# Eight k tiles of a feed-forward output projection as 2x2x2 block products with seven multiplications

## Chip, cores and metric

The kernel runs on one core of a Trainium2 chip. The metric is the device time of one execution in microseconds (us). All matrix products work in float32 accuracy: each operand is split into a high part, rounded for TensorE, and a low part, the remainder, and a product is made of three matmuls (high by high, high by low, low by high).

## What is computed

One layer of a decoder: a mixer sublayer (stick-breaking attention and a gated convolution), a cross-attention into 256 memory tokens, and a feed-forward sublayer (SwiGLU), each with a residual add, then a last RMSNorm. 512 tokens, 1024 channels, a hidden width of 2816. The change lies in the last product of the feed-forward sublayer:

```python
hf = rms_norm(x, norm_ffn[l])
gate, up = jnp.split(hf @ w_ffn_in[l], 2, axis=-1)
x = x + (jax.nn.silu(gate) * up) @ w_ffn_out[l]
...
return rms_norm(x, norm_final)
```

## The kernel before

Activations lie transposed: channels on the 128 partitions, 512 tokens along the free axis. A "tile" of channels is 128 of them: there are 8 tiles of model channels (`KD`) and 22 of the hidden width (`NF`).

**The tools of the kernel.** `load_w` brings a weight tile of 128x1024 by a DMA on SyncE's queue into a buffer `wr`, rounds it on ScalarE into `wh` (line 150) and takes the remainder on VectorE into `wl` (line 151). There are four buffers of each. `mm3` issues the three matmuls of a product (lines 155 to 157). `split` and `act_parts` make the high and low parts of activations, the cast on ScalarE, the remainder on VectorE. The buffers named `u` (50 of them, 128x512) hold activations and their forms.

**The input stage of the feed-forward sublayer** (up to about 729 us of the profile) already works with 2x2x2 blocks and seven products. A block is a pair of channel tiles by the two halves of the tokens (`HS` = 256) on one side and a pair of channel tiles by gate and up columns on the other. `forms_of` makes from two activation tiles the seven operands (sums and differences of quarters, VectorE, then split); `ffn_load` brings the weights of a block with three DMAs on SyncE's queue and one on GpSimd's that accumulates, so that two sums of weights are made by the DMA; `ffn_raw` makes two further sums on VectorE; `ffn_form` splits one operand into the buffers of `wh` and `wl` (which it shares with `load_w`): products 0 and 1 share a pair of buffers, the others take one buffer each, in turn from `wh` and from `wl`. `product` issues the twelve matmuls of 256 columns of one product (four k, three terms; line 803). Products 0, 3, 4 and 5 add up in one PSUM bank `z`; product 1 has a bank `v`; products 2 and 6 share a bank `y`. In between the values of `z` are copied out, since the outputs need partial sums of it.

The list `uses` gives the order over blocks m and products i: products of two neighbouring blocks alternate, so that between two products into the same `z` there is another one. The loop over it is hand-ordered on TensorE, ScalarE and VectorE (`manual_schedule`): these instructions keep their order among themselves, while instructions from outside the block may be put between them. At place n of the list the form of the product six places later is made (`AHEAD`) and the sum of the one eight places later (`SUM_AHEAD`).

**The output projection** (about 727 to 850 us) takes all eight PSUM banks as sums `acc[m]`, one for each tile of model channels: two from the pool of `v`, four from that of `z`, two from that of `y`; in the order m = 0 to 7 they are v, v, z, z, y, y, z, z. For each k tile, `out_step` issues for each m the three matmuls of 512 columns. That goes over the first 18 k tiles. The last four (`HOLD`) are held in all four weight buffers and worked half of the tokens by half (256 columns), in a hand-ordered block with the last norm and the output; its first nine products are the first three held tiles for m = 0 to 2. The residual `x2T[m]` (scaled beforehand, as the last norm is applied behind) is added there, when the sum of a half of one m is whole (line 983).

Of the kernel before, what the change touches and what calls it, by code (L numbers as in the profile page):

```python
# [11 lines left out]
ALU = mybir.AluOpType  # L12
# [14 lines left out]
HS = S // 2  # L27
EPS = 1e-6
HOLD = 4
MEM_AT = (5, 7, 9, 11)  # L30
MEAN_AT = 14
EARLY = 2
# [6 lines left out]

@with_exitstack  # L40
def hybrid_layer(ctx: ExitStack, tc: tile.TileContext, xT_d, memT_d, cols_d, wv_d, win_d,
                 wbr_d, wmix_d, wmq_d, wmk_d, wmv_d, wmo_d, wfi_d, wfo_d, out):
    nc = tc.nc

    cpool = ctx.enter_context(tc.tile_pool(name="cpool", bufs=1))
# [26 lines left out]
    def mmtile(s, pool=None, tag="mm"):  # L72
        return (pool or pmm).tile([P, 512], F32, tag=tag, name=nm(s))

    def ztile(s):
        return mmtile(s, pz, "z")
# [671 lines left out]

    def ffn_load(m):

        a = wfi_d[m].rearrange("p (i c) -> p i c", i=4)
        s13, wg = ((fpool, "wg") if (m % 3, t) in ((1, "ws"), (2, "wg")) else (wpool, "wr")
                   for t in ("ws", "wg"))
        s13 = s13[0].tile([P, 2, 512], F32, tag=s13[1], name=nm("ws"))
        nc.sync.dma_start(s13, a[:, 2:3, :].broadcast_to([P, 2, 512]))
        wg = wg[0].tile([P, 2, 512], F32, tag=wg[1], name=nm("wg"))
        nc.sync.dma_start(wg, a[:, 0:2, :])
        a22 = fpool.tile([P, 512], F32, tag="w2", name=nm("a22"), bufs=4)
        nc.sync.dma_start(a22, a[:, 3, :])
        nc.gpsimd.dma_start(s13, a[:, 0:4:3, :], accum_op=ALU.add)  # L760
        pairs[m] = wg
        raws[m] = [wg[:, 0, :], wg[:, 1, :], s13[:, 1, :], None, s13[:, 0, :], a22, None]
# [33 lines left out]
    def product(ps, m, i, ks=range(KP)):  # L796

        w = wforms[m, i]
        for k in ks:
            hi, lo = (w[j][:, k * P:(k + 1) * P] for j in range(2))  # L800
            xh, xl = x2f[k][i]
            for j, (a, b) in enumerate(((hi, xh), (hi, xl), (lo, xh))):
                nc.tensor.matmul(ps[:, :HS], a, b, start=i < 3 and k == 0 and j == 0,  # L803
                                 stop=k == KP - 1 and j == 2, skip_group_check=True)
# [43 lines left out]
                                                           in1=g[:, sl], op0=ALU.mult,  # L848
                                                           op1=ALU.mult))

    uses = [(0, 0), (0, 1), (0, 2)]
    for m in range(NF):
        if m < NF - 2:
            uses += [(m, 3), (m + 1, 0), (m, 4), (m + 1, 1), (m, 5), (m + 1, 2), (m, 6)]
        elif m == NF - 2:
            uses += [(m, 3), (m + 1, 0), (m, 4), (m + 1, 1), (m + 1, 2), (m + 1, 3), (m, 5),
                     (m + 1, 4), (m, 6), (m + 1, 5), (m + 1, 6)]
    actp = {}
    r2b = [None]

# [66 lines left out]
        evict(NF - 1, 2)  # L927


    acc = [mmtile("f") for _ in range(2)] + [ztile("f") for _ in range(4)]  # L930
    acc[4:4] = [otile("f") for _ in range(2)]

    def out_step(m, k, w, sl):
        fs = slice(m * P, (m + 1) * P)
        mm3(acc[m][:, sl], (w[0][:, 0, fs], w[1][:, 0, fs]), (actp[k][0][:, sl], actp[k][1][:, sl]),
            k == 0, k == NF - 1, skip_group_check=True)

    for k in range(NF - HOLD):
        w = load_w(wfo_d[k], D)
        if k + SCALED < NF:  # L940
            act_parts(k + SCALED, lows[-1:] + stts[-1:])
        for m in range(KD):
            out_step(m, k, w, slice(0, S))
    for k in range(NF - HOLD + SCALED, NF):
        act_parts(k, lows[-1:])
    held = [load_w(wfo_d[k], D) for k in range(NF - HOLD, NF)]
    tables = log_exp_tables(casts[-1])
    hs = HS
    halves = [slice(i * hs, (i + 1) * hs) for i in range(2)]
# [21 lines left out]
    with tc.manual_schedule(engines={mybir.EngineType.PE, mybir.EngineType.Activation,  # L971
                                     mybir.EngineType.DVE}):

        for m in range(3):
            for i in range(HOLD - 1):
                out_step(m, NF - HOLD + i, held[i], halves[0])
        for n in range(2 * KD):
            half, m = divmod(n, KD)
            sl = halves[half]
            for i in range(HOLD - 1 if n < 3 else 0, HOLD):  # L980
                out_step(m, NF - HOLD + i, held[i], sl)
            y = x2T[m][:, sl]
            nc.vector.tensor_tensor(out=y, in0=acc[m][:, sl], in1=y, op=ALU.add)
            if n > 0:
                add_square(*divmod(n - 1, KD))
            if n == 0:
                nc.vector.tensor_copy(v0, eps_sq[:, sl])
            elif n == KD:
                nc.vector.memset(v1, 0.0)
                parts = split(sq[0, 0], "sq", cols=hs)  # L990
            elif n == KD + 1:

                nc.vector.scalar_tensor_tensor(out=sq[1, 0], in0=eps_sq[:, sl], scalar=D / P,
                                               in1=sq[1, 0], op0=ALU.mult, op1=ALU.add)
            elif n == KD + 2:
                for i, part in enumerate(parts):
                    nc.tensor.matmul(v0, mean_r, part, start=False, stop=i == 1,
                                     skip_group_check=True)
            elif n == KD + 3:
                rf0 = rstd_of(v0, hs, "rf", tables, eps=False)  # L1000

            sq[half, m] = (acc[m][:, halves[0]] if half and 0 < m < KD - 2 else tmp("sq", hs))
            nc.scalar.activation(sq[half, m], y, AF.Square)
            if m % 2 == 0:
                yg[half, m // 2] = f(unit("yg")).rearrange("p (j t) -> p j t", j=2)
            nc.scalar.activation(yg[half, m // 2][:, m % 2, :], y, AF.Copy,
                                 scale=g_fin[:, m:m + 1])
        mean_of(0)
        mean_of(KD - 2)
        for m in range(2):  # L1010
            turn(m)
        mean_of(KD - 1)
        for m in range(2, KD):
            turn(m)
        r1 = rstd_of(v1.rearrange("p (c two) -> p c two", two=2)[:, :, 0], 2, "rt", tables,
                     eps=False)
        for j in range(2):
            for c in range(2):
                o, ps = f(unit("out")), acc[2 * j + c]
                if c == 0:  # L1020
                    nc.scalar.activation(o, ps, AF.Copy, scale=r1[:, 0:1])
                else:
                    nc.vector.tensor_scalar(out=o, in0=ps, scalar1=r1[:, 1:2], scalar2=None,
                                            op0=ALU.mult)
                q = nc.scalar if (j, c) == (1, 0) else nc.sync
                q.dma_start(out[1].rearrange("(c p d) -> c p d", c=2, d=D)[
                    c, :, j * 512:(j + 1) * 512], o)
# [12 lines left out]
def _layout(x, mem, norm_mix, w_in, conv_w, w_branch_a, w_branch_b, w_mix_out, norm_mem_q,  # L1040
            norm_mem_kv, w_mem_q, w_mem_kv, w_mem_o, norm_ffn, w_ffn_in, w_ffn_out, norm_final):
    import numpy as np

    def by_column(w, cols=P, k=KD):

        n = w.shape[1] // cols
        return w.reshape(k, P, n, cols).transpose(2, 1, 0, 3).reshape(n, P, k * cols)

    def by_row(w):

        return w.reshape(4, 2, P, 512).transpose(0, 2, 1, 3).reshape(4, P, 1024)

    def by_pair(w):


        return w.reshape(KD // 2, 2, P, 2, NF, P).transpose(4, 2, 3, 1, 0, 5).reshape(NF, P, 2048)

    gains = np.stack([norm_mix[0], norm_mem_q[0], norm_mem_kv[0], norm_ffn[0], norm_final])
    columns = np.concatenate([gains.reshape(5 * KD, P), conv_w[0].reshape(3 * TT, P)])
    arrays = {  # L1060
        "xT": x[0].T,
        "memT": mem[0].T,
        "columns": columns.T,
        "w_value": by_row(w_in[0][:, O_V:O_V + SBW]),
        "w_in": by_column(w_in[0]),
        "w_branch": np.concatenate([by_column(w_branch_a[0], k=4), by_column(w_branch_b[0], k=4)],
                                   axis=2),
        "w_mix_out": by_column(w_mix_out[0]),
        "w_mem_q": by_column(w_mem_q[0]),
        "w_mem_k": by_column(w_mem_kv[0][:, :D]),  # L1070
        "w_mem_v": np.stack([by_row(w_mem_kv[0][:, D + 512 * n:D + 512 * (n + 1)])
                             for n in range(2)]),
        "w_mem_o": by_column(w_mem_o[0]),
        "w_ffn_in": by_pair(w_ffn_in[0]),
        "w_ffn_out": w_ffn_out[0].reshape(NF, P, D),
    }
    return {f"in_{n}_dram": np.ascontiguousarray(a) for n, a in arrays.items()}

# [17 lines left out]
```

## Time and profile before

| | us |
|---|---|
| median of 3 runs | 859.74 (859.27 to 860.23) |
| the profiled execution, its own time | 859.25 |
| its span, first to last instruction | 857.5 |
| TensorE busy | 850.1 |
| VectorE busy | 585.9 |
| ScalarE busy | 430.7 |

The profile is one execution. PE is TensorE's matmuls, PEld its weight loads (beside the matmuls), DVE is VectorE, ACT ScalarE, POOL GpSimd, SP SyncE. "L803" is line 803 of the kernel. A group of instructions reads: line, engine, operation, output<-input tile, shapes, count | busy us in all, mean ns of one | idle time of the engine just before them and what ended it. In the timeline the first two numbers are start and length in us; neighbouring instructions of one engine overlap by a little, so the distance of two starts is what an instruction costs in a row, and the length is somewhat more.

### The profile page before, as it was taken

How to read it: one execution, taken by the hardware profiler on the slowest of the kernel's cores; microseconds unless marked ns; L12 is line 12 of the kernel's file. 1: busy time of each engine (PE TensorE's matmuls, PEld its weight loads, DVE VectorE, ACT ScalarE, POOL GpSimd, SP SyncE). 2: the span in 40 equal slices, each digit the busy share in tenths (PEclk: the TensorE clock that was granted, in tenths of full speed). 3: DMA queues.
4: the chain of work that ended last, by engine and by line, in shares of the span. 5: the costliest groups of instructions: out<-in, count | busy, mean ns of one | idle time of the engine just before them, and what ended most of it. 6: DMA issues, size and time to landing. Idle time of an engine off the chain costs nothing.

```text
span 857.5 us, 12690 instructions
## 1 busy us (share of the span) xinstructions
PE 850.1 (99%) x4912; PEld 748.4 (87%) x4912; DVE 585.9 (68%) x963; ACT 430.7 (50%) x750; POOL 64.5 (8%) x92
## 2 busy tenths in 40 slices
PE   9999999999999999999999999999999999999997
PEld 7878787888888898888888889999999999888897
DVE  9769889986454475555555789888877778533334
ACT  7465767664233344433434666554455556422335
POOL 1011112210000000000000101111111100000002
PEclk9999999999999999999999999999999999999999
DMA  8332232219333255333120527777777764332202
GB/s 296 134 112 87 87 111 87 74 59 296 112 105 112 91 172 191 128 98 99 50 74 25 142 56 196 192 176 176 189 185 195 181 147 135 111 99 99 73 1 99
DMA packets 42859, 108.34 MB, mean 126 GB/s; under 512 B 4656, under 2 KB 8752, under 8 KB 42800
## 3 DMA queue, kind: packets, MB, share of 16 engines
q1 hardware_dynamic: 36528, 95.72, 34.1%
q0 software_dynamic: 5984, 11.54, 8.3%
q8 instruction: 38, 0.62, 0.3%
q10 hardware_dynamic: 288, 0.29, 0.1%
q14 instruction: 21, 0.17, 0.1%
HBM read 104.36 MB, written 2.10 MB: 124 GB/s over the span
## 4 chain that ended last, share of the span: by engine, by line
PE 99%; DVE 0%; POOL 0%; issue 0%; DVEq 0%; ACT 0%; POOLq 0%
PE z L803 15%; PE pr L155 8%; PE pr L156 8%; PE pr L157 8%; PE y L803 7%; PE f L156 5%; PE f L155 5%; PE f L157 5%; PE v L803 4%; PE r L157 3%; PE r L156 3%; PE r L155 3%; PE v L261 3%; PE mq L157 2%; PE mq L155 2%; PE mq L156 2%
## 5 line engine op out<-in xcount | busy, mean ns | idle before, releaser
L150 ACT CAST wh<-wr 128x1024 fp32r<-128x1024 f32 x106 | 111.2, 1052 | 218.4 <-issue 98.6
L151 DVE TENSOR_TENSOR wl<-wr,wh 128x1024 fp32r<-128x1024 f32 x106 | 129.2, 1221 | 99.5 <-ACT wh L150 99.2
L155 PE MATMUL pr<-xgh,wh 128*128 128x512 f32 x288 | 112.6, 391 | 0.0
L156 PE MATMUL pr<-xgl,wh 128*128 128x512 f32 x288 | 112.3, 390 | 0.0
L157 PE MATMUL pr<-xgh,wl 128*128 128x512 f32 x288 | 112.3, 390 | 0.0
L156 PE MATMUL f<-actl,wh 128*128 128x512 f32 (+1 forms) x208 | 74.2, 357 | 0.0
L155 PE MATMUL f<-acth,wh 128*128 128x512 f32 (+1 forms) x208 | 74.2, 357 | 0.0
L157 PE MATMUL f<-acth,wl 128*128 128x512 f32 (+1 forms) x208 | 74.0, 357 | 0.0
L803 PE MATMUL z<-xdh,wf 128*128 128x256 f32 x352 | 70.3, 283 | 0.0
L157 PEld LDWEIGHTS pr<-xgh,wl 128*128 128x128 f32 x288 | 54.1, 188 | 11.4
L155 PEld LDWEIGHTS pr<-xgh,wh 128*128 128x128 f32 x288 | 54.1, 188 | 11.2 <-DVE rv L124 0.3
L156 PEld LDWEIGHTS pr<-xgl,wh 128*128 128x128 f32 x288 | 54.1, 188 | 10.8
L760 POOL DMA_DIRECT2D ws<-in_w_ffn_in_dram x22 | 26.6, 1208 | 468.0 <-DVE c L618 266.3
L803 PEld LDWEIGHTS z<-xdh,wf 128*128 128x128 f32 x352 | 58.0, 192 | 0.0
L823 ACT COPY sa<-z 128x256 f32<-128x256 f32 x44 | 16.4, 373 | 78.2 <-PE z L803 78.2
L803 PE MATMUL z<-xdl,wf 128*128 128x256 f32 x176 | 49.8, 283 | 0.0
L794 DVE TENSOR_TENSOR wf<-s,wf 128x512 fp32r<-128x512 f32 x44 | 30.3, 690 | 21.1 <-ACT wf L793 20.0
L155 PEld LDWEIGHTS f<-acth,wh 128*128 128x128 f32 x208 | 39.3, 189 | 5.8
L157 PEld LDWEIGHTS f<-acth,wl 128*128 128x128 f32 x208 | 39.3, 189 | 5.6
L156 PEld LDWEIGHTS f<-actl,wh 128*128 128x128 f32 x208 | 39.3, 189 | 5.5
L803 PE MATMUL y<-xch,wf 128*128 128x256 f32 x176 | 35.5, 283 | 0.0
L803 PE MATMUL v<-xoh,wf 128*128 128x256 f32 x176 | 35.5, 283 | 0.0
(281 smaller groups left out, 2135.5 us busy)
## 6 DMA issues: line engine op xcount, KB each, us to landing
wr<-in_w_in_dram SPq DMA_DIRECT2D x36, 512.0 KB, 3.4
ws<-in_w_ffn_in_dram SPq DMA_DIRECT2D x22, 512.0 KB, 3.8
wg<-in_w_ffn_in_dram SPq DMA_DIRECT2D x22, 512.0 KB, 4.3
ws<-in_w_ffn_in_dram POOLq DMA_DIRECT2D x22, 512.0 KB, 5.8
wr<-in_w_ffn_out_dram SPq DMA_DIRECT2D x22, 512.0 KB, 3.3
a<-in_w_ffn_in_dram SPq DMA_DIRECT2D x22, 256.0 KB, 4.5
wr<-in_w_branch_dram SPq DMA_DIRECT2D x8, 512.0 KB, 3.3
wr<-in_w_mem_k_dram SPq DMA_DIRECT2D x8, 512.0 KB, 3.3
```

The lines of the kernel that those rows point to most:

```text
L150: after(nc.scalar.copy(h2, raw), lead[-1:])
L151: lows.append(nc.vector.tensor_tensor(out=l2, in0=raw, in1=f(h2), op=ALU.subtract))
L155: nc.tensor.matmul(ps, a[0], b[0], start=start, stop=False, **kw)
L156: nc.tensor.matmul(ps, a[0], b[1], start=False, stop=False, **kw)
L157: nc.tensor.matmul(ps, a[1], b[0], start=False, stop=stop, **kw)
L261: nc.tensor.matmul(vps[t], xg[k][a][:, sl], wv[k][b], start=k == 0 and (a, b) == (0, 0), stop=k == KD - 1 and a == 1)
L760: nc.gpsimd.dma_start(s13, a[:, 0:4:3, :], accum_op=ALU.add)
L794: nc.vector.tensor_tensor(out=lo, in0=raw, in1=f(hi), op=ALU.subtract)
L803: nc.tensor.matmul(ps[:, :HS], a, b, start=i < 3 and k == 0 and j == 0, stop=k == KP - 1 and j == 2, skip_group_check=True)
L823: nc.scalar.copy((s[:, :HS], None, None, s[:, HS:], t[:, :HS])[i], z)
```

## The change

K tiles 10 to 17 of the output projection leave the plain loop, which now runs over the first ten (`TURN`). They become four pairs (`NT`) of k tiles; the eight output tiles become four pairs (`NB`); the tokens two halves. Each block, numbered 22 to 25 as a continuation of the blocks of the input stage, is one pair of output tiles over all four k pairs, in seven products with the same `product`, `ffn_form`, `ffn_raw` and `ffn_load`; the weights come from a new array laid out by blocks. The operands of the activations, `af`, are made by `forms_of` at k = 2, 4, 6 and 8 of the plain loop.

Behind the plain loop come the parts of the four held activation tiles and the first six places of the new order. Then, hand-ordered: eight adds move the sums of ten k tiles out of the banks into `x2T`; 28 products follow, each with a `part_of`, which adds its bank (or subtracts it) to one quarter of the block in `x2T`. Afterwards the eight banks are taken anew, the four held weight tiles are loaded, and the tail runs as before over the held tiles, now beginning new sums.

```diff
+TURN = 10
+NT = (NF - HOLD - TURN) // 2
+NB = D // (2 * P)
...
-        a = wfi_d[m].rearrange("p (i c) -> p i c", i=4)
+        a = (wfi_d[m] if m < NF else wfp_d[m - NF]).rearrange("p (i c) -> p i c", i=4)
...
-            xh, xl = x2f[k][i]
+            xh, xl = (x2f if m < NF else af)[k][i]
...
+    def order(m0, n):
+        u = [(m0, 0), (m0, 1), (m0, 2)]
+        for m in range(m0, m0 + n - 2):
+            u += [(m, 3), (m + 1, 0), (m, 4), (m + 1, 1), (m, 5), (m + 1, 2), (m, 6)]
+        m = m0 + n - 2
+        return u + [(m, 3), (m + 1, 0), (m, 4), (m + 1, 1), (m + 1, 2), (m + 1, 3), (m, 5),
+                    (m + 1, 4), (m, 6), (m + 1, 5), (m + 1, 6)]
+
+    uses = order(0, NF)
+    af = []
...
-    for k in range(NF - HOLD):
+    for k in range(TURN):
         w = load_w(wfo_d[k], D)
-        if k + SCALED < NF:
+        if k + SCALED < TURN:
             act_parts(k + SCALED, lows[-1:] + stts[-1:])
+        if k > 1 and k % 2 == 0 and len(af) < NT:
+            j = TURN + 2 * len(af)
+            af.append(forms_of(act[j], act[j + 1]))
         for m in range(KD):
-            out_step(m, k, w, slice(0, S))
-    for k in range(NF - HOLD + SCALED, NF):
+            out_step(m, k, w, slice(0, S), 0, TURN - 1)
+    for k in range(NF - HOLD, NF):
         act_parts(k, lows[-1:])
-    held = [load_w(wfo_d[k], D) for k in range(NF - HOLD, NF)]
+
+    def part_of(m, i):
+
+        z, v, y = (banks[m][t][:, :HS] if t in banks[m] else None for t in "zvy")
+        xa, xb = x2T[2 * (m - NF)], x2T[2 * (m - NF) + 1]
+        x, ps, sign = {0: (xa[:, :HS], z, 1), 1: (xa[:, :HS], v, 1), 2: (xb[:, HS:], y, -1),
+                       3: (xa[:, HS:], z, 1), 4: (xb[:, HS:], z, -1), 5: (xb[:, :HS], z, -1),
+                       6: (xa[:, HS:], y, 1)}[i]
+        if sign > 0:
+            nc.vector.tensor_tensor(out=x, in0=ps, in1=x, op=ALU.add)
+        else:
+            nc.vector.scalar_tensor_tensor(out=x, in0=ps, scalar=-1.0, in1=x, op0=ALU.mult,
+                                           op1=ALU.add)
+
+    turns = order(NF, NB)
+    for n in range(AHEAD):
+        ffn_form(*turns[n])
+    with tc.manual_schedule(engines={mybir.EngineType.PE, mybir.EngineType.Activation,
+                                     mybir.EngineType.DVE}):
+        for m in range(KD):
+            nc.vector.tensor_tensor(out=x2T[m], in0=acc[m], in1=x2T[m], op=ALU.add)
+        for n, (m, i) in enumerate(turns):
+            if i < 3:
+                banks.setdefault(m, {})["zvy"[i]] = (ztile, mmtile, otile)[i]("zvy"[i])
+            product(banks[m]["zvyzzzy"[i]], m, i)
+            part_of(m, i)
+            if n + AHEAD < len(turns):
+                ffn_form(*turns[n + AHEAD])
+            if n + AHEAD + SUM_AHEAD < len(turns):
+                ffn_raw(*turns[n + AHEAD + SUM_AHEAD])
+
+    acc = out_banks()
+    held = [load_w(wfo_d[TURN + i], D) for i in range(HOLD)]
     tables = log_exp_tables(casts[-1])
```

In the tail, `out_step` begins its sums at the first held tile instead of continuing them. The host lays `w_ffn_out` out as the 14 plain k tiles and, in `w_ffn_turn`, the four blocks.

More of the change, by code (lines that the diff above doesn't have):

```diff
@@ L41, in hybrid_layer @@
 def hybrid_layer(ctx: ExitStack, tc: tile.TileContext, xT_d, memT_d, cols_d, wv_d, win_d,
-                 wbr_d, wmix_d, wmq_d, wmk_d, wmv_d, wmo_d, wfi_d, wfo_d, out):
+                 wbr_d, wmix_d, wmq_d, wmk_d, wmv_d, wmo_d, wfi_d, wfo_d, wfp_d, out):
     nc = tc.nc
@@ L849, in evict @@
                                                            op1=ALU.mult))
[L851 to L857, printed above, removed]
+    def order(m0, n):
[7 more added lines that the diff above has]
+    af = []
     actp = {}
@@ L927, in hybrid_layer, with out_banks, out_step @@
         evict(NF - 1, 2)
-    acc = [mmtile("f") for _ in range(2)] + [ztile("f") for _ in range(4)]
-    acc[4:4] = [otile("f") for _ in range(2)]
-    def out_step(m, k, w, sl):
+    def out_banks():
+        acc = [mmtile("f") for _ in range(2)] + [ztile("f") for _ in range(4)]
+        acc[4:4] = [otile("f") for _ in range(2)]
+        return acc
+    acc = out_banks()
+    def out_step(m, k, w, sl, first, last):
         fs = slice(m * P, (m + 1) * P)
         mm3(acc[m][:, sl], (w[0][:, 0, fs], w[1][:, 0, fs]), (actp[k][0][:, sl], actp[k][1][:, sl]),
-            k == 0, k == NF - 1, skip_group_check=True)
@@ L938, in hybrid_layer @@
-    for k in range(NF - HOLD):
+            k == first, k == last, skip_group_check=True)
+    for k in range(TURN):
         w = load_w(wfo_d[k], D)
-        if k + SCALED < NF:
+        if k + SCALED < TURN:
             act_parts(k + SCALED, lows[-1:] + stts[-1:])
+        if k > 1 and k % 2 == 0 and len(af) < NT:
+            j = TURN + 2 * len(af)
+            af.append(forms_of(act[j], act[j + 1]))
         for m in range(KD):
-            out_step(m, k, w, slice(0, S))
-    for k in range(NF - HOLD + SCALED, NF):
+            out_step(m, k, w, slice(0, S), 0, TURN - 1)
@@ L947, in hybrid_layer @@
+    acc = out_banks()
+    held = [load_w(wfo_d[TURN + i], D) for i in range(HOLD)]
     tables = log_exp_tables(casts[-1])
@@ L975, in hybrid_layer @@
             for i in range(HOLD - 1):
-                out_step(m, NF - HOLD + i, held[i], halves[0])
+                out_step(m, NF - HOLD + i, held[i], halves[0], NF - HOLD, NF - 1)
         for n in range(2 * KD):
@@ L980, in hybrid_layer @@
             for i in range(HOLD - 1 if n < 3 else 0, HOLD):
-                out_step(m, NF - HOLD + i, held[i], sl)
+                out_step(m, NF - HOLD + i, held[i], sl, NF - HOLD, NF - 1)
             y = x2T[m][:, sl]
@@ L1056, in by_pair, with by_block @@
         return w.reshape(KD // 2, 2, P, 2, NF, P).transpose(4, 2, 3, 1, 0, 5).reshape(NF, P, 2048)
+    def by_block(w):
+        return w.reshape(NT, 2, P, NB, 2, P).transpose(3, 2, 4, 1, 0, 5).reshape(NB, P, 2048)
     gains = np.stack([norm_mix[0], norm_mem_q[0], norm_mem_kv[0], norm_ffn[0], norm_final])
@@ L1074, in _layout @@
         "w_ffn_in": by_pair(w_ffn_in[0]),
-        "w_ffn_out": w_ffn_out[0].reshape(NF, P, D),
+        "w_ffn_out": w_ffn_out[0].reshape(NF, P, D)[list(range(TURN)) +
+                                                    list(range(NF - HOLD, NF))],
+        "w_ffn_turn": by_block(w_ffn_out[0][TURN * P:(NF - HOLD) * P]),
     }
```

## The prediction

> **What bounds the kernel now.** I read the page first: busy times, then the chain that ended last.
>
> ```profile
> PE 850.1 (99%) x4912; PEld 748.4 (87%) x4912; DVE 585.9 (68%) x963; ACT 430.7 (50%) x750; POOL 64.5 (8%) x92
> PE 99%; DVE 0%; POOL 0%; issue 0%; DVEq 0%; ACT 0%; POOLq 0%
> ```
>
> TensorE is busy for 99% and it is 99% of the chain. So the kernel gets shorter only if TensorE's matmul stream gets shorter, and it gets longer by every hole put into that stream. The second view is the busy time by stretch: the feed-forward input stage, eight k tiles of the output projection, its last four k tiles, and the end.
>
> ```profile
> core 0: us, PE busy (x) PEld busy (x) DVE busy (x) ACT busy (x) POOL busy (x), PEclk, DMA share, GB/s
> 520.22:721.79 201.57, 201.57 (x1681) 201.57 (x1681) 167.76 (x297) 110.82 (x208) 21.64 (x18) 1.00 0.69 175
> 743.84:787.32 43.48, 43.48 (x193) 36.03 (x192) 14.61 (x16) 12.60 (x17) 0.00 (x0) 1.00 0.30 97
> 825.40:852.00 26.60, 26.45 (x223) 26.18 (x221) 14.93 (x40) 15.57 (x39) 5.02 (x4) 1.00 0.12 40
> 852.00:857.50 5.50, 0.00 (x0) 0.00 (x0) 1.09 (x2) 0.93 (x2) 0.00 (x0) 0.74 0.51 193
> ```
>
> TensorE has no hole in either stage that matters, at full clock. The output projection leaves VectorE two thirds free (14.61 of 43.48 us); the input stage, which already works with seven products, uses it for 167.76 of 201.57 us. Its matmul stream still has no hole, so that pattern of work fits behind TensorE there.
>
> **The price of a matmul in each form.** The third view is the timeline and the chain. First one k tile of the projection (24 matmuls of 512 columns): the cast of a weight tile starts when TensorE has read the tile that lay there before, so casts mark the period. Below them a block of products (84 matmuls of 256 columns) as the chain shows it.
>
> ```profile
> 814.52 1.05 ACT L150 CAST wh<-wr 128x1024 fp32r<-128x1024 f32 x1 [4.38 <-PE f L156]
> 819.96 1.05 ACT L150 CAST wh<-wr 128x1024 fp32r<-128x1024 f32 x1 [4.38 <-PE f L156]
> 530.27 4.32 PE z L803 x36
> 534.59 1.44 PE v L803 x12
> 536.03 1.44 PE z L803 x12
> 537.47 2.88 PE y L803 x24
> 540.35 4.32 PE z L803 x36
> ```
>
> A k tile takes 819.96 - 814.52 = 5.44 us, which is 226.7 ns a matmul. A block takes 540.35 - 530.27 = 10.08 us, which is 120 ns a matmul, 1.44 us a product of twelve. Two half-width matmuls cost 240 ns, 6% more than one of full width. This is where the naive count goes wrong: seven products for eight promise an eighth of 43.5 us, 5.4 us, but the pieces are of the dearer form.
>
> **Main term.** Removed: k tiles 10 to 17, 8 x 5.44 = 43.52 us (192 matmuls). Added: 4 blocks x 7 products x 1.44 = 40.32 us (336 matmuls). Gain 3.2 us. The bounds of it: at half the full-width price, 113.3 ns, the 336 would take 38.1 us and the gain be 5.4; dearer than 120 ns they are nowhere in this trace. I take 120 ns, since shape, operands and code (line 803) are those of the input stage. [...]
>
> **VectorE in the new stage.** Prices: each product is now added to the residual by a VectorE instruction that reads PSUM (`part_of`), 28 of 128x256; ahead of them stand eight adds of 128x512 that move the ten-tile sums out. Near rows:
>
> ```profile
> L833 DVE TENSOR_TENSOR sb<-y,sb 128x256 f32<-128x256 f32 x22 | 9.2, 416 | 0.0
> L847 DVE SCALAR_TENSOR_TENSOR act<-z,fg 128x256 f32<-128x256 f32 x22 | 9.2, 416 | 1.3 <-ACT fg L842 1.3
> L646 DVE TENSOR_TENSOR x<-r,x 128x512 f32<-128x512 f32 x16 | 11.0, 690 | 26.9 <-PE r L157 26.9
> L785 DVE TENSOR_TENSOR wf<-wg,wf 128x1024 fp32r<-128x1024 f32 x22 | 26.9, 1224 | 11.6 <-ACT wf L784 11.5
> L794 DVE TENSOR_TENSOR wf<-s,wf 128x512 fp32r<-128x512 f32 x44 | 30.3, 690 | 21.1 <-ACT wf L793 20.0
> L771 DVE TENSOR_TENSOR s<-s,wg 128x512 f32<-128x512 f32 x22 | 15.0, 682 | 0.0
> 598.32 0.68 DVE L794 TENSOR_TENSOR wf<-ws,wf 128x512 fp32r<-128x512 f32 x1
> 598.92 0.42 DVE L847 SCALAR_TENSOR_TENSOR act<-z,fg 128x256 f32<-128x256 f32 x1
> 599.26 0.41 DVE L847 SCALAR_TENSOR_TENSOR act<-sb,fg 128x256 f32<-128x256 f32 x1
> ```
>
> A block costs at most 7 x 0.42 (adds) + 1.22 (paired form) + 5 x 0.69 (single forms) + 2 x 0.68 (sums) = 9.0 us of 10.08. The timeline rows show that neighbours overlap (0.60 us from start to start for 128x512, 0.34 for 128x256), so about 8 us. That is the load of the input stage, whose PSUM reads stand partly on ScalarE. The wait to watch: z of a block gathers four products and is read between them, so the next z product waits for the add of the one before it. The order leaves at least one other product (1.44 us) between; a slot with two other VectorE jobs holds 0.34 + 0.60 + 0.60 = 1.54 us, which pushes the next add by 0.1 us. Behind a waiting add on VectorE stands only the split of a form that is used six products later. Cost: zero. With that cover gone (VectorE a slot late) it would be the lateness itself.
>
> **The forms and loads made earlier.** The operand forms (`forms_of`) of eight act tiles are, each of four times, 5 VectorE jobs of 128x256 and 3 of 128x512, 5 x 0.42 + 3 x 0.69 = 4.2 us; with the first weight forms (2 x 1.22 + 4 x 0.69 = 5.2 us) 22 us. They lie beside the ten k tiles (54.4 us), where VectorE is two thirds idle by the stretch above. Zero. The weights of a block are 1.75 MB in four transfers against 1 MB in two, one of them issued by POOL with accumulation; the four blocks stand in SP's queue ahead of the last four weight tiles.
>
> ```profile
> ws<-in_w_ffn_in_dram POOLq DMA_DIRECT2D x22, 512.0 KB, 5.8
> wr<-in_w_ffn_out_dram SPq DMA_DIRECT2D x22, 512.0 KB, 3.3
> POOL yg L1031 <- DVE rf L131: 150.1, 1, 150.1
> ```
>
> A block is needed every 10.08 us, as in the input stage (DMA share 0.69); POOL stands idle for those 150 us. The buffers of the held tiles' raw weights come free at the latest with the last sum of block 25, at product 19 of 27, 11.5 us before the stage ends, for 3.3 us of landing. Zero.
>
> **The two seams.** These are the unknown, since before has no such place. *In:* the first product needs the bank of output tile 2, the third of the eight adds. TensorE sums the tiles one after the other (5.44 / 8 = 0.68 us each), an add starts every 0.60 us, so the third is long done when the last tile ends. *Out:* each held tile's weights need slots of `wh` and `wl`, which now come free one after the other at the ends of products 21, 23, 25 and 27. The casts and splits have to be finished by the time of use.
>
> ```profile
> 825.20 0.39 PE L157 MATMUL f<-acth,wl 128*128 128x512 f32 x1
> 825.42 0.28 PE L155 MATMUL f<-acth,wh 128*128 128x256 f32 x1
> 826.48 1.23 DVE L151 TENSOR_TENSOR wl<-wr,wh 128x1024 fp32r<-128x1024 f32 x1 [4.21 <-ACT wh L150]
> 829.22 0.42 DVE L983 TENSOR_TENSOR x<-f,x 128x256 f32<-128x256 f32 x1 [1.51 <-PE f L157]
> L793 ACT CAST wf<-s 128x512 fp32r<-128x512 f32 x44 | 27.4, 622 | 2.5 <-DVE s L771 2.5
> ```
>
> Before, the tail starts at 825.42 and the fourth held tile is split until 827.71, needed 27 x 0.12 = 3.24 us after the start: covered by the first three. Now the third is free 2.9 us before the seam and needs 1.22; the fourth is free at the seam and, behind one add (0.42), done 1.7 us later. Both fit if VectorE takes them between the last adds, which leave it idle for 1.1 us in each of the last six slots. The far ends are 3.0 us at the entry and 2.9 at the exit (rivals); the near end is zero, not less, for the chain holds no wait there that could go. I take 0.2 us for both together, as at the old tail's seam, where the first add began at 829.22, right behind the thirty matmuls it needs (825.42 + 30 x 0.12 = 829.02). Sum: 859.25 (span 857.5) - 3.2 + 0.2 = 856.25 for the profiled execution; the median of before lies 0.49 higher, so **856.7 us**.
>
> **Rivals.** *One seam eats the gain (859.4).* If VectorE's splits of the held tiles stand behind the last product's add, the third is ready 0.42 + 3 x 1.14 = 3.84 us after it (1.14 is 1.22 less the overlap), and TensorE needs it after 8 matmuls, 0.96 us: 2.9 us idle, 859.74 - 3.2 + 2.9. *Slower: VectorE keeps the written order at both seams (862.4).* Then at the entry a weight form stands ahead of the adds: that of product (22, 4), whose slot is that of k tile 9 and comes free only when TensorE ends that tile. Cast 0.62, split 0.69, three adds of 0.60: TensorE idles 3.0 us; with 2.9 at the exit the sum is 859.74 - 3.2 + 5.9 = 862.4. It decides as soon as both seams together cost over 4.9 us. For it: the diff writes those forms ahead of the adds, and the held loads after all products. Against it, VectorE's queue at an older seam:
>
> ```profile
> 721.71 0.68 DVE L869 TENSOR_TENSOR actl<-act,acth 128x512 fp32r<-128x512 f32 x1
> 722.31 2.35 DVE L151 TENSOR_TENSOR wl<-wr,wh 128x1024 fp32r<-128x1024 f32 x2
> 724.95 0.42 DVE L828 TENSOR_TENSOR fg<-y,sa 128x256 f32<-128x256 f32 x1 [0.28 <-PE y L803]
> 725.29 1.21 DVE L151 TENSOR_TENSOR wl<-wr,wh 128x1024 fp32r<-128x1024 f32 x1
> 726.42 0.68 DVE L840 TENSOR_TENSOR fg<-fg,r0b 128x512 f32<-128x512 f32 x1
> ```
>
> Splits of loads (L151), written behind the whole hand-ordered block, stand between its instructions: the program's queues follow readiness, not the written order. Idle of that length could cost clock as well: where TensorE had no work, in 852 to 857.5, the granted clock was 0.74. [...] *Cheaper products (854.5):* a matmul costs by its columns alone, the half price of the main term, 859.74 - 5.4 + 0.2; the 120 ns of all blocks of the input stage speak against it. *That the change doesn't do what it says:* that VectorE, not TensorE, bounds the new stage; 9.0 of 10.08 us speaks against it, and I give it nothing of its own.
>
> **How the numbers follow.** A difference below 0.2% (1.7 us) can't be told from none. Forecast 0.65 (own range 856.0 to 858.0: seams of 0 to 1.3, and the spread of the runs), cheaper products 0.04, one seam 0.18, both seams 0.13. So faster 0.69, same 0.18, slower 0.13. The range takes in one seam and the forecast and leaves out the slower case and the far end of the cheaper one: 855.5 to 860.0.
>
> **What would show it.** Right: matmuls of line 803's product in groups of twelve at 1.44 us through 40.3 us, ten periods of 5.44 us ahead of them, 80 instead of 144 full-width matmuls in each of the three `f` groups, no TensorE idle over 0.3 us at either seam, splits of held tiles between the last adds, span about 854.5. Wrong: TensorE waiting for a split of a held tile or for one of the eight adds (a seam), or for `part_of` between z products (VectorE a slot late), or a product longer than 1.44 us.

## The result and the profile after

The changed kernel takes 857.1 us (median of 7 runs, 856.29 to 858.39) against 859.73 us for the kernel before (7 runs, 859.27 to 860.36): a ratio of 0.9971 with a 95% interval of 0.9959 to 0.9982, 2.6 us faster. The profiled execution took 856.29 us with a span of 854.6; the prediction had 856.25 and about 854.5.

The page and the chain of the kernel after, to set beside those of before: TensorE is still 99% of the chain, with 3.2 us less to do.

```profile
PE 846.9 (99%) x5056; PEld 752.7 (88%) x5056; DVE 622.2 (73%) x1047; ACT 441.6 (52%) x774; POOL 69.4 (8%) x96
PE 99%; DVE 0%; POOL 0%; issue 0%; DVEq 0%; ACT 0%; POOLq 0%
```

Busy time by stretch, after: the whole stage of the products, and three blocks of its middle (columns as in the prediction).

```profile
782.04:822.36 40.32, 40.32 (x338) 40.32 (x338) 32.49 (x60) 16.68 (x24) 1.20 (x1) 1.00 0.38 105
786.35:816.59 30.24, 30.24 (x255) 30.24 (x254) 25.09 (x47) 13.01 (x19) 1.20 (x1) 1.00 0.46 124
```

TensorE has no hole in the new stage, its weight loads (PEld) none either, and VectorE is busy for 25.09 of 30.24 us, 8.4 us a block. The chain of the same kernel, with start and length: from the last plain matmul to the last product, first and last pieces.

```profile
781.59 0.23 PE f L159
782.04 1.43 PE z L806 x12
783.47 1.44 PE v L806 x12
784.91 1.44 PE y L806 x12
786.35 4.32 PE z L806 x36
...
818.05 1.44 PE y L806 x12
819.49 1.44 PE z L806 x12
820.93 1.44 PE y L806 x12
```

28 products begin at 782.04 and are through at 822.37: 40.33 us, 1.44 each. VectorE's timeline at the two seams, after:

```profile
777.32 0.69 DVE L979 TENSOR_TENSOR x<-f,x 128x512 f32<-128x512 f32 x1 [4.40 <-PE f L160]
777.93 1.22 DVE L788 TENSOR_TENSOR wf<-wg,wf 128x1024 fp32r<-128x1024 f32 x1
779.06 3.67 DVE L979 TENSOR_TENSOR x<-f,x 128x512 f32<-128x512 f32 x6
782.65 0.68 DVE L797 TENSOR_TENSOR wf<-ws,wf 128x512 fp32r<-128x512 f32 x1
783.25 0.68 DVE L979 TENSOR_TENSOR x<-f,x 128x512 f32<-128x512 f32 x1
783.85 0.41 DVE L968 TENSOR_TENSOR x<-z,x 128x256 f32<-128x256 f32 x1
...
814.69 1.22 DVE L154 TENSOR_TENSOR wl<-wr,wh 128x1024 fp32r<-128x1024 f32 x1
815.83 0.41 DVE L968 TENSOR_TENSOR x<-z,x 128x256 f32<-128x256 f32 x1
816.63 0.42 DVE L970 SCALAR_TENSOR_TENSOR x<-z,x 128x256 f32<-128x256 f32 x1 [0.39 <-PE z L806]
816.97 1.22 DVE L154 TENSOR_TENSOR wl<-wr,wh 128x1024 fp32r<-128x1024 f32 x1
...
819.87 1.22 DVE L154 TENSOR_TENSOR wl<-wr,wh 128x1024 fp32r<-128x1024 f32 x1
...
822.75 1.22 DVE L154 TENSOR_TENSOR wl<-wr,wh 128x1024 fp32r<-128x1024 f32 x1
```

At the entry the adds (L979) follow TensorE's last plain tile, and the form of product 4 (782.65), written ahead of them, stands between the seventh and the eighth. At the exit three of the four splits of the held tiles (L154) stand between the last `part_of` (L968, L970), one behind every second product; the fourth comes right behind the last of them (822.75) and is done 1.6 us after the products end. Both are the interleaving that the prediction counted on.

The last VectorE instruction of the chain, before and then after:

```profile
851.68 0.75 DVE out L1023
```

```profile
848.48 0.75 DVE out L1068
```

It comes 3.20 us earlier. The spans differ by 2.9, since the output's last transfer ended 6.1 us behind that instruction and not 5.8. So the computation gained the 3.2 us of the main term; why the medians differ by less is taken up under "What is left".

### The profile page after: what moved, and what is told of

Same layout as the page of the kernel before. It is cut to its first block, busy times and chain, and to the rows that moved or that the text cites. A ratio compares the mean times of both kernels' runs of the same rounds, so it can differ in the third digit from the quotient of the medians.

```text
span 854.6 us, 13139 instructions
## 1 busy us (share of the span) xinstructions
PE 846.9 (99%) x5056; PEld 752.7 (88%) x5056; DVE 622.2 (73%) x1047; ACT 441.6 (52%) x774; POOL 69.4 (8%) x96
## 4 chain that ended last, share of the span: by engine, by line
PE 99%; DVE 0%; POOL 0%; issue 0%; DVEq 0%; ACT 0%; POOLq 0%
PE z L806 18%; PE y L806 9%; PE pr L158 8%; PE pr L160 8%; PE pr L159 8%; PE v L806 4%; PE r L160 3%; PE r L158 3%; PE r L159 3%; PE f L159 3%; PE f L158 3%; PE f L160 3%; PE v L264 3%; PE mq L160 2%; PE mq L158 2%; PE br L158 2%
## 5 line engine op out<-in xcount | busy, mean ns | idle before, releaser
L154 DVE TENSOR_TENSOR wl<-wr,wh 128x1024 fp32r<-128x1024 f32 x98 | 119.4, 1221 | 41.1 <-ACT wh L153 40.8
L806 PE MATMUL z<-xdh,wf 128*128 128x256 f32 x416 | 83.0, 283 | 0.0
L806 PEld LDWEIGHTS z<-xdh,wf 128*128 128x128 f32 x416 | 68.4, 192 | 0.0
L806 PE MATMUL z<-xdl,wf 128*128 128x256 f32 x208 | 58.8, 283 | 0.0
L159 PE MATMUL f<-actl,wh 128*128 128x512 f32 (+1 forms) x144 | 49.3, 342 | 0.0
L158 PE MATMUL f<-acth,wh 128*128 128x512 f32 (+1 forms) x144 | 49.3, 342 | 0.0
L160 PE MATMUL f<-acth,wl 128*128 128x512 f32 (+1 forms) x144 | 49.1, 342 | 0.0
L796 ACT CAST wf<-ws 128x512 fp32r<-128x512 f32 x52 | 31.9, 617 | 20.3 <-PE f L159 8.8
L788 DVE TENSOR_TENSOR wf<-wg,wf 128x1024 fp32r<-128x1024 f32 x26 | 31.8, 1224 | 14.1 <-ACT wf L787 14.0
L806 PE MATMUL z<-xf,wf 128*128 128x256 f32 x312 | 41.8, 283 | 0.0
```

Of the source, the lines that this page charges most:

```text
L154: lows.append(nc.vector.tensor_tensor(out=l2, in0=raw, in1=f(h2), op=ALU.subtract))
L158: nc.tensor.matmul(ps, a[0], b[0], start=start, stop=False, **kw)
L159: nc.tensor.matmul(ps, a[0], b[1], start=False, stop=False, **kw)
L160: nc.tensor.matmul(ps, a[1], b[0], start=False, stop=stop, **kw)
L788: nc.vector.tensor_tensor(out=lo, in0=pair, in1=f(hi), op=ALU.subtract)
L796: nc.scalar.copy(hi, raw)
```

## The experiments

All times beside a run name are medians of its runs; the kernel before stood at 859.8 to 860.2 us beside them.

**The changed kernel again.** No edit.

> The changed kernel once more, to see how far its runs lie apart and whether a second profile shows a slower execution. Stream theory (the gain is 8 x 5.44 us less 28 x 1.44 us of TensorE and nothing else): 856.3 to 857.1 us, the tail beginning 3.2 us earlier than in the kernel before, 822.2 us. Rival (now and then something in the new stage comes late, a transfer or VectorE): if this execution is one of 857 us or more, its trace has a hole in TensorE's matmuls between 782 and 822 us that the first trace has not; if it is the same hole as elsewhere in the kernel, the new stage is not the cause.

857.0 us (856.36 to 857.55), ratio 0.997 [0.9958, 0.9981]. Its trace is the first one again: span 854.6 us, no hole in the products, the last one ending at 822.42. An execution of 857 us or more was not profiled here, so this run says nothing of the rival; what is known of the spread stands under "What is left".

**Half-width matmuls without products.** In the kernel before:

```diff
         for m in range(KD):
-            out_step(m, k, w, slice(0, S))
+            for sl in [slice(0, HS), slice(HS, S)] if k >= 10 else [slice(0, S)]:
+                out_step(m, k, w, sl)
```

> The kernel before, with the matmuls of k tiles 10 to 17 split into two of 256 columns: same columns, twice the instructions, no products. Stream theory with a price of 120 ns: 384 x 0.120 = 46.1 us in place of 43.5, so 2.6 us slower, 862.3 us, a k tile 5.76 us. Rival (a matmul costs by its columns alone, and the 120 ns of the input stage come from what else runs there): no change, 859.7 us, a k tile 5.44 us.

862.18 us, ratio 1.0029 [1.0018, 1.004], 2.4 us slower. The period of its k tiles is visible in the casts; the first gap belongs to a plain tile, the next to halves:

```profile
777.01 1.05 ACT L150 CAST wh<-wr 128x1024 fp32r<-128x1024 f32 x1 [3.87 <-PE f L156]
782.45 1.05 ACT L150 CAST wh<-wr 128x1024 fp32r<-128x1024 f32 x1 [3.87 <-PE f L156]
...
794.07 1.05 ACT L150 CAST wh<-wr 128x1024 fp32r<-128x1024 f32 x1 [4.19 <-PE f L156]
799.83 1.05 ACT L150 CAST wh<-wr 128x1024 fp32r<-128x1024 f32 x1 [4.19 <-PE f L156]
```

5.44 us and 5.76 us: 226.7 and 120 ns a matmul, in the same place, with the same operands. The price of the form is shown by itself, and with it the 2.2 us by which the gain falls short of an eighth of 43.5 us.

**Quarter-width matmuls.** In the kernel before, over k tiles 10 to 13:

```diff
-            out_step(m, k, w, slice(0, S))
+            n = P if 10 <= k < 14 else S
+            for c in range(0, S, n):
+                out_step(m, k, w, slice(c, c + n))
```

> The kernel before, with the matmuls of k tiles 10 to 13 split into four of 128 columns. Why does a matmul of 256 columns cost 120 ns and not half of 226.7? First theory: each matmul pays the same 13.3 ns on top of 0.417 ns a column (213.3 + 13.3 and 106.7 + 13.3); then 128 columns cost 66.7 ns, a k tile 96 x 66.7 = 6.4 us in place of 5.44, the kernel 3.8 us more, 863.6 us. Second theory: at 256 columns the weight load of each matmul (busy without a gap in the input stage) sets the pace; then 128 columns cost 120 ns as well, a k tile 11.5 us, the kernel 24.3 us more, 884 us.

881.48 us (one run), 21.7 us more. TensorE's timeline of that stretch:

```profile
789.82 0.27 PE L157 MATMUL f<-acth,wl 128*128 128x128 f32 x1
...
792.95 0.27 PE L155 MATMUL f<-acth,wh 128*128 128x128 f32 x1
```

28 matmuls between 789.82 and 792.95 give 112 ns each. So halving the columns once more saves 8 ns of 120. The first theory (66.7 ns) falls; the second is near, though its floor is 112 and not 120 ns. That the weight load sets the floor would fit, since PEld is busy for all of the 20 us from 785 to 805, but PEld is as busy at 256 columns (40.32 of 40.32 us in the new stage), where a matmul takes 120 ns, and the load was not tried by itself. The cause of the floor stays open.

**The entry seam alone.** In the kernel before (`out_banks` takes the eight banks anew):

```diff
...
+        if k == 10:
+            for m in range(KD):
+                nc.vector.tensor_tensor(out=x2T[m], in0=acc[m], in1=x2T[m], op=ALU.add)
+            acc = out_banks()
...
-            k == 0, k == NF - 1, skip_group_check=True)
+            k in (0, 10), k in (9, NF - 1), skip_group_check=True)
```

> The entry seam alone: the kernel before, with eight adds after ten k tiles that move the sums into the residual, and k tiles 10 to 17 as plain as they were, in new sums. Stream theory: the adds (0.60 us each) follow TensorE's 0.68 us a tile and each bank is free 4 us before it is needed, so no change, 859.8 us. Rival (moving the sums costs TensorE time): up to the eight adds, 4.8 us, 864.6 us.

859.67 us, ratio 0.9999 [0.999, 1.0008]. Moving the sums out costs nothing, as its adds trail TensorE tile by tile: in the trace seven of them take 4.27 us in a row, TensorE waits nowhere in the projection (its one wait of the run, 1.6 us, is that of the kernel before on line 220), and the span is 857.5 us, as in the kernel before.

**The exit in the written order.** In the changed kernel (`last` is the last `part_of`, `after` sets an order on one engine):

```diff
...
-    held = [load_w(wfo_d[TURN + i], D) for i in range(HOLD)]
+    held = []
+    for i in range(HOLD):
+        held.append(load_w(wfo_d[TURN + i], D))
+        after(lows[-1], [last])
```

> The changed kernel, with the four splits of the held weight tiles ordered behind VectorE's last add of a product. Theory that the interleaving of these splits is what keeps the exit seam closed: TensorE idles 2.9 us at the exit (0.42 + 3 x 1.14 - 0.96), 860.0 us, so the whole gain is gone to within 0.3 us. Rival (the tail has slack of its own and takes the delay up later, or TensorE's other matmuls run ahead): 857.1 us.

860.52 us (859.51 to 862.56), ratio to the kernel before 1.0012 [1.0004, 1.0021]. The runs fall into two groups, six at 859.5 to 859.9, with a mean granted clock of 0.998 or 0.999, and six at 861.2 to 862.6, with 0.995 to 0.997. The profiled execution is one of the upper group. Its TensorE timeline at the seam, then busy time by stretch with the granted clock (the last three numbers: clock, DMA share, GB/s):

```profile
822.71 0.28 PE L158 MATMUL f<-acth,wh 128*128 128x256 f32 x1
822.83 0.28 PE L159 MATMUL f<-actl,wh 128*128 128x256 f32 x1
824.52 0.39 PE L160 MATMUL f<-acth,wl 128*128 128x256 f32 x1 [1.41 <-DVE wl L154]
...
825.65 0.58 PE L160 MATMUL f<-acth,wl 128*128 128x256 f32 x1 [0.51 <-DVE wl L154]
...
826.79 0.58 PE L160 MATMUL f<-acth,wl 128*128 128x256 f32 x1
```

```profile
824.50:826.80 2.30, 1.64 (x7) 1.14 (x7) 2.30 (x3) 0.00 (x0) 0.00 (x0) 0.69 0.00 0
826.80:829.00 2.20, 2.20 (x10) 2.20 (x11) 1.07 (x1) 0.00 (x0) 0.00 (x0) 0.50 0.00 0
829.00:831.00 2.00, 2.00 (x11) 2.00 (x10) 0.00 (x0) 0.00 (x0) 0.00 (x0) 0.50 0.00 0
831.00:832.50 1.50, 1.50 (x9) 1.50 (x9) 0.58 (x2) 0.15 (x1) 0.00 (x0) 0.60 0.00 0
832.50:834.00 1.50, 1.50 (x15) 1.50 (x14) 1.35 (x4) 1.50 (x5) 0.00 (x0) 1.00 0.00 0
```

The ninth matmul, the low part of the third tile, starts at 826.79 where 822.71 + 8 x 0.12 = 823.67 was its time: 3.1 us late, as worked out (2.9). The lower group shows that: 859.6 less 857.0 is 2.6 us, the gain gone to within 0.2 us of the kernel before. The upper group loses 1.6 to 3 us more: in its profile TensorE runs at half clock from 825.4 to 832.2, where a matmul takes 0.21 in place of 0.12 us.

**A short hole at the exit.** As above, but only for the third and fourth tile (`if i > 1: after(...)`).

> The exit seam with a short hole: only the splits of the third and fourth held tile are ordered behind VectorE's last add. The third is then ready 0.55 + 1.22 = 1.8 us after the last product and needed after 0.96, so TensorE idles 0.8 to 0.9 us: 857.9 us. Theory that the half clock needs a long hole: no execution shows it, all lie within 857.2 to 858.6 us. Rival (any hole near a second costs clock now and then): some executions 2 us or more above the others.

857.76 us (857.28 to 858.47), ratio to the kernel before 0.9972 [0.9962, 0.9983]: 0.8 us over the changed kernel's 857.0. TensorE waits 0.7 us by the trace, and no execution of eight shows a second group; the mean granted clock is 0.998 or more in all of them.

**The entry in the written order.** In the changed kernel (`low` is the split of the form of product 4):

```diff
...
-            nc.vector.tensor_tensor(out=x2T[m], in0=acc[m], in1=x2T[m], op=ALU.add)
+            add = nc.vector.tensor_tensor(out=x2T[m], in0=acc[m], in1=x2T[m], op=ALU.add)
+            if m == 0:
+                after(add, low)
```

> The changed kernel, with the eight adds ordered behind the split of the form of product 4 of the first block, whose buffer comes free only with the end of k tile 9. Theory: TensorE idles 3.0 us at the entry (cast 0.62, split 0.69, three adds of 0.60), 860.1 us. Rival (the products wait for more than the third add, since VectorE is late for the first reads of z as well): up to 4.5 us, 861.6 us. Second rival (no effect): 857.1 us.

862.02 us (859.91 to 864.26), ratio to the kernel before 1.0022 [1.0013, 1.0032]. The chain at the seam:

```profile
781.96 0.62 ACT wf L796
782.61 0.69 DVE wf L797
783.30 0.66 DVE x L981 x2
783.96 0.45 issue
784.41 0.69 DVE x L981
785.11 0.14 issue
785.24 1.81 PE z L808 x12
787.05 2.56 PE v L808 x12
```

Cast, split, three adds: the chain that the prediction wrote down for this rival, and a wait of 3.10 us by the trace against 3.0. Behind it product 1 takes 2.56 in place of 1.44 us, at a granted clock of 0.50 (787.0 to 788.5). Four runs lie at 859.9 to 860.7, with a mean granted clock of 0.998 or 0.999; six at 861.4 to 862.7 and two at 863.9 to 864.3, with 0.995 to 0.997.

**Both at once.**

> Both seams in the written order at once: the slower rival of the prediction. By holes alone 857.0 + 3.1 + 2.9 = 863.0 us (the two single runs, where the clock held). Theory that a hole of 3 us can also cost clock, in some executions and not in others: 862.6 to 868 us, in groups about 2 to 3 us apart, each group one spell of half clock more. Rival (holes add up and nothing else): 862.6 to 863.4 us in all executions.

Three executions took 865.06, 865.75 and 867.68 us (a fourth, at 1704 us, is left out, and so is one of 1400 us of the kernel before in the same series); ratio to the kernel before 1.0071 [1.0055, 1.0086]. Each is over the 863.0 us that the holes alone would give; in the profiled one the clock falls behind both holes (means of 0.66 over 786 to 791 us and of 0.64 over 830 to 833).

**Room on VectorE.** In the changed kernel:

```diff
             part_of(m, i)
+            nc.vector.tensor_copy(tmp("dummy", HS), banks[m]["zvyzzzy"[i]][:, :HS])
```

> The changed kernel, with one idle copy of 128x256 out of PSUM behind each product's add on VectorE, 28 in all, to see how much room is left there. VectorE is busy for 32.5 of the stage's 40.3 us and the copies ask for 28 x 0.34 = 9.5 more, 42.0. Theory that VectorE is the next bound and close: TensorE has to wait 1.7 to 3 us in all, 858.7 to 860 us, in holes ahead of products that add to z. Rival (VectorE is far from the bound): 857.0 us.

858.27 us (857.46 to 859.62), 1.3 us over the changed kernel; ratio to the kernel before 0.9983 [0.9974, 0.9993]. The stretch from 782 to 823 us, VectorE 39.58 of 41.00:

```profile
782.00:823.00 41.00, 40.30 (x334) 39.95 (x333) 39.58 (x86) 16.43 (x24) 1.20 (x1) 1.00 0.36 104
```

VectorE is the next bound, but the 9.5 us of added work cost 1.2 us of TensorE. The products end at 823.77, 1.4 us later, but 0.24 of that are two matmuls of the tail that ran among them (817.77); the span is 855.8 us instead of 854.6. That is under the 1.7 to 3 us expected. TensorE's two short waits (0.35 us each by the trace) are ahead of z products and put off what follows by 0.58 us each. The trace names ScalarE's cast as what ended them; but by the program such a product reads a form cast six places earlier, while it writes the bank z that VectorE's copy was still reading. The copy ends 0.15 us ahead of both starts (at 789.45 and 800.11), about the 0.14 us that lay between add and product at the entry in the written order. So it was most likely the copy. It also holds its bank longer than the add alone, so the room for work that does not read PSUM may be a little wider than this run shows.

**A candidate with three held tiles.** `HOLD = 3`, `TURN = 11` in the changed kernel.

> A candidate: the changed kernel with three held k tiles in place of four and eleven plain ones in place of ten, so that one k tile more runs at full width. Stream theory: 48 matmuls at 120 ns become 24 at 226.7, 5.76 against 5.44 us, so 0.3 us faster, 856.7 us, the tail beginning 5.44 us later and being 5.76 us shorter. Rival: the tail's steps shrink from 1.44 to 1.08 us of TensorE and no longer cover the add, the square and the scaled copy (0.34 + 0.32 + 0.46 us), or the three held tiles come late: 857.0 us or more, up to 16 x 0.1 us above.

857.01 us (856.78 to 857.95), ratio to the kernel before 0.997 [0.9959, 0.9982], no better than the changed kernel. In its trace the tail's matmuls take 5.8 us less, as expected, but from their end to the last VectorE instruction it is 3.6 us in place of 2.8: the scale of the last norm, which VectorE makes, is now in the chain between the last transposes and that instruction. That takes back more than the 0.3 us. The changed kernel stays the best of those run.

## Why the prediction was right

**Main term.** 8 x 5.44 us gone, 28 x 1.44 us come, gain 3.2 us: the trace has 40.33 us for the products and the last VectorE instruction 3.20 us earlier. The choice of 120 ns over the half price was the one that mattered, and the run with half-width matmuls alone shows it. Measured were 226.7, 120 and 112 ns at 512, 256 and 128 columns; by the columns alone, a half and a quarter of the first, the others would be 113.3 and 56.7.

**VectorE.** "About 8 us" a block, at most 9.0: 8.4 measured, and the idle copies bear out that the cover was some 8 us wide over the stage (40.3 less 32.5): 9.5 us of added work cost 1.2. No z product waited.

**The seams.** Allowed 0.2 us, measured none. Why they are closed is the part that could have been luck, and the orders forced on the chip show it is the interleaving: with the written order at the exit 3.1 us are lost (2.9 worked out), at the entry 3.10 (3.0). Either cancels the gain. That the profiled execution met its forecast to 0.04 us is partly luck: the 0.2 us for the seams was not used, and the last transfer came 0.3 us later, which was not forecast.

**What was wrong in a rival.** The slower rival was priced at 862.4 us by its holes, and forcing both orders measured 865.1 to 867.7. The step that failed is the sum: the prediction says that idle of that length could cost clock, and its 862.4 has no term for it. It does cost clock, in half of the executions at the exit and in eight of twelve at the entry, 1 to 4 us each time. The profiled execution at the entry took 862.0 us against 860.3, the middle of the four without; by the clock of its stretches, shown in the last section, it lost 1.7 us (1.80 x 0.11 + 1.50 x 0.50 + 1.10 x 0.50 + 2.40 x 0.09 = 1.71, an estimate).

**What is left.** The medians gained 2.6 and 2.8 us in the two comparisons, not 3.2. Part of the difference is made at the beginning of an execution. The cast that starts at 33.86 us in the profile of before starts within 0.1 us of that in seven of the twelve profiles, that of after (33.85) among them, and 0.5 to 1.2 us later in the other five (34.43 in that of the halves, 34.64 in that of the three held tiles, 35.06 in that of the short hole), though the code is the same there. Behind it they run in step: the short hole's profile is 1.21 us behind that of after at this cast and 1.22 us behind at the last product but one (820.71 against 819.49). The spans of the seven runs of the changed kernel lie 1.2 us apart as well (854.6 to 855.8). That is enough for most of the spread of the runs, and a gain of 3.2 us lies inside the intervals; what makes the beginning later in some executions was not looked for.

## What to carry to other kernels

Price seven products for eight with the cost of a matmul of the smaller form, read from a stage that already runs it: here half the columns cost 53% and a quarter 49%, so the gain was 7% of the stage and not 12.5%, and by these prices a second level would lose (an estimate, 7/8 x 2 x 112 = 196 ns in place of 120; no run tried it). At a seam between two such stages, look whether the engines beside TensorE take its work in the order of readiness: the same instructions in the written order turned the gain into a loss (860.5 and 862.0 us against 859.8). And price a hole in TensorE with the clock that may go with it, not by its length alone: behind holes of 3.1 us that was 1 to 4 us here, in 14 of 24 executions.

## What the runs showed of the hardware

A hole of about 3.1 us in TensorE's work was followed by half the granted clock in some executions of the same program and not in others: in eight of twelve at the entry and in six of twelve at the exit, going by the mean granted clock of each run (0.995 to 0.997 against 0.998 or 0.999). At the exit the hole was in parts: waits of 1.41, 0.51 and less, with matmuls between them. A hole of 0.7 us did it in none of eight (0.998 or more). Why a hole of the same length lost clock in some executions and not in others was not shown.

Busy time by stretch of the profiled execution with the entry in the written order (the last three numbers: clock, DMA share, GB/s), then of the one with both orders forced:

```profile
782.00:785.20 3.20, 0.15 (x1) 0.00 (x0) 2.59 (x5) 1.09 (x2) 0.00 (x0) 1.00 0.24 65
785.20:787.00 1.80, 1.76 (x13) 1.79 (x14) 1.80 (x4) 0.00 (x0) 0.00 (x0) 0.89 0.53 175
787.00:788.50 1.50, 1.50 (x9) 1.50 (x8) 1.42 (x3) 0.00 (x0) 0.53 (x1) 0.50 0.00 1
788.50:789.60 1.10, 1.10 (x7) 1.10 (x6) 0.00 (x0) 0.16 (x1) 0.67 (x1) 0.50 0.00 0
789.60:792.00 2.40, 2.40 (x21) 2.40 (x20) 2.31 (x5) 1.08 (x2) 0.00 (x0) 0.91 0.86 126
```

```profile
786.00:791.00 5.00, 5.00 (x32) 5.00 (x31) 3.68 (x8) 0.62 (x1) 1.20 (x1) 0.66 0.28 36
791.00:826.00 35.00, 35.00 (x294) 35.00 (x293) 25.63 (x50) 14.18 (x21) 0.00 (x0) 1.00 0.33 104
826.00:830.00 4.00, 2.12 (x16) 1.72 (x14) 2.98 (x5) 0.91 (x1) 0.00 (x0) 1.00 0.00 0
830.00:833.00 3.00, 2.44 (x11) 2.23 (x12) 2.27 (x3) 0.00 (x0) 0.00 (x0) 0.64 0.00 0
833.00:836.00 3.00, 3.00 (x23) 3.00 (x22) 0.51 (x2) 0.08 (x1) 0.00 (x0) 0.79 0.00 0
```

At the entry the granted clock was 1.00 in the hole, 0.89 over the 1.80 us in which TensorE resumed (785.24 us), 0.50 over the next 2.60 us, with TensorE busy for all of them, and 0.91 behind. With both forced it was 0.66 and 0.64 behind the two holes and 1.00 over the 35 us between them.

A matmul of 128 columns, with its own weight load, took 112 ns (181 matmuls and 181 loads in 20 us), barely less than one of 256 (120 ns).
